# A block of expert_u in one transfer and two buffers instead of two transfers and three buffers; picks worked in place

## Chip, cores and metric

The kernel runs on one core of a Trainium2 chip. The metric is the device time of one execution in microseconds (us); a kernel's time is the median of its runs.

## What is computed

One inference step of a one-layer hybrid decoder: adaLN, an input projection, dilated attention on eight heads and RWKV-7 on eight others, an output projection, and then a layer of product-key experts (PEER), which is the part that matters here. For 1024 prompt tokens and 32 sample tokens of width 1024:

```python
q = (hb @ w_pq).reshape(chunk, PEER_HEADS, 2, PEER_HALF)
s = jnp.einsum('nhpc,hpkc->nhpk', q, sub_keys).astype(jnp.float32)
s1, i1 = lax.top_k(s[:, :, 0], PEER_TOPK)
s2, i2 = lax.top_k(s[:, :, 1], PEER_TOPK)
cand = (s1[..., :, None] + s2[..., None, :]).reshape(chunk, PEER_HEADS, PEER_TOPK * PEER_TOPK)
cid = (i1[..., :, None] * PEER_KEYS + i2[..., None, :]).reshape(chunk, PEER_HEADS, PEER_TOPK * PEER_TOPK)
top_s, pos = lax.top_k(cand, PEER_TOPK)
eid = jnp.take_along_axis(cid, pos, axis=-1)
gate = jax.nn.softmax(top_s, axis=-1)
act = jax.nn.gelu(jnp.einsum('nd,nhkd->nhk', hb, expert_u[eid]).astype(jnp.float32), approximate=False)
return jnp.einsum('nhk,nhkd->nd', gate * act, expert_v[eid].astype(jnp.float32))
```

There are 16384 experts; expert_u and expert_v are 64 MB each in float32. All of it is computed in float32.

## The kernel before

The first 1690 us are the projections, attention, RWKV and the picks of most tokens. The program then works on two things at once.

**The dense loop** (`dense`) treats prompt tiles 0 to 4 (640 tokens) by running all 16384 experts in 128 blocks of 128. `hidden(b)` loads a block of expert_u, transposed, as two halves of [128, 512] floats into the tile u (three buffers of 2 KB a partition), through SP's queue. `split2` makes two float32r operands of each half: ACT casts it to uh, and POOL subtracts, ul = u - uh. uh and ul have two buffers, each for a whole block. PE then multiplies the block with the tokens (h2T), 48 matmuls of 320 columns; ACT takes the gelu, DVE multiplies with the gates g, which SP loads for four blocks at a time (two loads of 640 KB to a group, in rows of 512 B), and ch and cl are the split result. Four blocks are a group. `values` loads a half of the width of expert_v for four blocks (v, two buffers of 2 KB a partition) and splits it into vh (ACT) and vl (POOL, every eighth on DVE), with five buffers each; `output` sums a group's four blocks for one token tile and half of the width, 12 matmuls of 512 columns, and DVE adds the result to dacc. There are ten outputs to a group and 32 groups. In the last group an output is followed by its end: SP loads x1 into the tile fx (which shares the tag and so the buffers of u), DVE multiplies with a gate and adds, SP stores to y.

**The routed tiles**, 5, 6, 7 and the sample tile, take only the experts picked for each token. Their scores come from `route_scores` (weights wq_d through the tile w, five buffers for the tiles 6, 7 and sample), the picks from `route_pick`, and then 832 gathers (`gathered`), each an indirect DMA that POOL issues, of 128 rows of 4 KB of expert_u or expert_v into one of five buffers of the tile row. DVE takes the dot products with expert_u, and sums the rows of expert_v (into gh or ga).

`route_pick` turns the indices of the two top-16 lists into floats (fi, tile tf), adds them to codes cid (tile td), takes the top 16 (tile tt) with their places pu (tile tp), shifts the places into pf (tile te), and subtracts on POOL to find the picked code (tile tq).

The order on each engine is set before the run by the framework's scheduler, which goes by priorities, buffers and its own costs: the gathers and routed tiles are woven with the dense loop, and a change of a buffer count can move instructions of all engines. Each engine then works strictly in that order, and a DMA on SP that waits for a buffer holds all that stand behind it. In the profile every operation has line 196, the recording layer, so instructions go by their tiles' names.

## Time and profile before

| | |
|---|---|
| runs, us | 3748.92, 3759.01, 3769.43; median 3759.01 |
| profiled execution, us | 3753.1 |
| its span, us | 3751.3 |
| mean granted TensorE clock | 0.967 |
| PE busy | 3453.9 us (92%) |
| DVE busy | 2693.2 us (72%) |
| POOL busy | 2080.6 us (55%) |
| ACT busy | 1431.2 us (38%) |
| DMA | 981.58 MB, mean 262 GB/s |

The span is the time from the first to the last instruction of the execution that was profiled; its own time is 1.8 us longer. Shares are means over the span, and the stages have different limits: the dense loop, about 2050 us, has PE and the DMA engines both busy over nine tenths, so what ends each wait there has to be read from that stretch. PE's time is kept apart from that of its weight loads (PEld), which overlap with the matmuls. A busy PE includes the tail of a matmul in the pipeline, and the granted clock is either whole (2.4 GHz) or half of it, so a mean of 0.99 in a stretch is a few us at the lower level.

### The profile page before, as it was taken

The numbers are of one execution on the slowest core, as the hardware profiler recorded it, in microseconds if no ns is written. First come the engines' busy times: TensorE is split into PE (matmuls) and PEld (weight loads), VectorE is DVE, ScalarE is ACT, GpSimd is POOL, SyncE is SP. The second block draws the span as 40 slices with busy tenths as digits, with TensorE's granted clock in tenths as the row PEclk, the third lists the DMA queues.
The fourth block names the chain that finished last, engine by engine and source line by source line (L and its number), as shares of the span: only waits on it lengthen the run. The fifth ranks groups of instructions, "written<-read, shape, count | busy, mean of one in ns | idle before, by whom it ended". The sixth has DMA issues, their size and how long they took to land.

```text
span 3751.3 us, 57270 instructions
## 1 busy us (share of the span) xinstructions
PE 3453.9 (92%) x19618; PEld 2873.9 (77%) x19618; DVE 2693.2 (72%) x6059; ACT 1431.2 (38%) x3122; POOL 2080.6 (55%) x1842
## 2 busy tenths in 40 slices
PE   7999999789888988988999989999999999999998
PEld 3878678567767755556777778988888888898997
DVE  2556365588688656785778998787777877777787
ACT  5645345336765754543221122322223222222321
POOL 2342011015545446754655677777777777776784
PEclk8999999899999989998999999999999999999999
DMA  9653596553675568749988779999999999999997
GB/s 293 197 148 117 176 285 186 151 182 130 225 233 166 189 229 255 244 149 309 320 316 298 262 255 334 340 321 322 327 323 324 329 320 322 315 330 318 336 336 256
DMA packets 592528, 981.58 MB, mean 262 GB/s; under 512 B 78323, under 2 KB 354620, under 8 KB 589420
## 3 DMA queue, kind: packets, MB, share of 16 engines
q1 hardware_dynamic: 467788, 524.84, 43.9%
q0 software_dynamic: 124448, 453.08, 34.1%
q8 instruction: 155, 2.54, 0.3%
q14 instruction: 137, 1.12, 0.1%
HBM read 882.97 MB, written 94.78 MB: 261 GB/s over the span
## 4 chain that ended last, share of the span: by engine, by line
PE 51%; DMA 18%; DVE 14%; issue 7%; POOL 6%; ACT 3%; SPq 1%; POOLq 0%; DVEq 0%; ACTq 0%
PE d L196 23%; PE at L196 10%; PE rw L196 5%; PE pj L196 5%; DMA u<-in_uT 5%; PE rs L196 3%; POOL row L196 3%; DMA row<-in_expert_v,eid 3%; PE sp L196 2%; POOL vl L196 2%; DVE gh L196 2%; DVE ohb L196 1%; DMA v<-in_expert_v 1%; DMA w<-wq_d 1%; POOL ul L196 1%
## 5 line engine op out<-in xcount | busy, mean ns | idle before, releaser
L196 PE MATMUL d<-h2T,uh 128*128 128x320 f32 x4096 | 907.3, 311 | 18.1 <-DVE cl L196 9.0
L196 PEld LDWEIGHTS d<-h2T,uh 128*128 128x128 f32 x4096 | 689.6, 189 | 26.6 <-ACT h2T L196 8.2
L196 PE MATMUL d<-h2T,ul 128*128 128x320 f32 x2048 | 633.3, 311 | 0.6 <-POOL ul L196 0.6
L196 PE MATMUL d<-vl,ch 128*128 128x512 f32 x1280 | 508.3, 398 | 42.9 <-POOL vl L196 42.9
L196 DVE CUSTOM_DVE_ANT_0 row<-row,gh 128x1024 f32<-128x1024 f32 x416 | 500.4, 1215 | 63.5 <-DMA row<-in_expert_u,eid 50.7
L196 POOL DMA_INDIRECT row<-in_expert_u,eid x416 | 394.7, 949 | 242.0 <-DVE co L196 89.6
L196 PE MATMUL d<-vh,cl 128*128 128x512 f32 x1280 | 504.5, 395 | 0.0
L196 PE MATMUL d<-vh,ch 128*128 128x512 f32 x1280 | 478.3, 396 | 17.2 <-DVE cl L196 9.7
L196 POOL DMA_INDIRECT row<-in_expert_v,eid x416 | 397.1, 955 | 166.2 <-issue 46.2
L196 POOL TENSOR_SCALAR oha<-c_iota,tr 128x128 f32<-128x128 f32 x320 | 307.4, 966 | 312.1 <-PE sp L196 293.6
L196 POOL TENSOR_TENSOR ul<-u,uh 128x512 fp32r<-128x512 f32 x256 | 332.2, 1306 | 151.7 <-ACT uh L196 143.3
L196 ACT CAST vh<-v 128x512 fp32r<-128x512 f32 x256 | 158.8, 622 | 674.9 <-DMA v<-in_expert_v 451.9
L196 DVE SCALAR_TENSOR_TENSOR gh<-row,co,gh 128x1024 f32<-128x1024 f32 x285 | 366.1, 1285 | 48.6 <-DMA row<-in_expert_v,eid 46.7
L196 PEld LDWEIGHTS d<-h2T,ul 128*128 128x128 f32 x2048 | 386.2, 189 | 5.0 <-issue 3.7
L196 POOL TENSOR_TENSOR wl<-w,wh 128x1024 fp32r<-128x1024 f32 x50 | 123.0, 2461 | 387.2 <-ACT wh L196 326.8
L196 PEld LDWEIGHTS d<-vl,ch 128*128 128x128 f32 x1280 | 244.1, 191 | 108.0 <-POOL vl L196 58.6
L196 POOL TENSOR_TENSOR vl<-v,vh 128x512 fp32r<-128x512 f32 x224 | 289.0, 1301 | 45.7 <-ACT vh L196 42.7
L196 PEld LDWEIGHTS d<-vh,ch 128*128 128x128 f32 x1280 | 242.7, 190 | 77.5 <-DVE dacc L196 12.7
L196 ACT CAST uh<-u 128x512 fp32r<-128x512 f32 x256 | 154.8, 621 | 367.3 <-DMA u<-in_uT 212.2
L196 PEld LDWEIGHTS d<-vh,cl 128*128 128x128 f32 x1280 | 243.9, 191 | 52.8 <-issue 2.5
L196 DVE TENSOR_TENSOR dacc<-dacc,d 128x512 f32<-128x512 f32 x310 | 206.2, 683 | 47.8 <-PE d L196 47.6
L196 DVE TENSOR_TENSOR d<-d,g 128x320 f32<-128x320 f32 x256 | 126.8, 496 | 155.6 <-ACT d L196 142.4
(449 smaller groups left out, 6779.4 us busy)
## 6 DMA issues: line engine op xcount, KB each, us to landing
u<-in_uT SPq DMA_DIRECT2D x256, 256.0 KB
v<-in_expert_v SPq DMA_DIRECT2D x256, 256.0 KB
w<-wq_d SPq DMA_DIRECT2D x224, 256.0 KB
g_d<-stage SPq DMA_DIRECT2D x20, 2048.0 KB
g<-g_d SPq DMA_DIRECT2D x64, 640.0 KB
w<-in_w_in SPq DMA_DIRECT2D x75, 512.0 KB
w<-in_w_out SPq DMA_DIRECT2D x112, 256.0 KB
adaw<-in_ada_w SPq DMA_DIRECT2D x32, 512.0 KB
```

Of the source, the lines that this page charges most:

```text
L196: return f(*a, **k)
```

## The change

A block of expert_u comes in one transfer of [128, 1024] floats, 4 KB a partition, into two buffers (8 KB in place of 6). ACT's casts and POOL's subtractions stay in halves. The end of the last group, whose fx has the same tag, then has two buffers too. `route_pick` keeps the float indices in the place of the integer ones (ti) and the shifted places in pu, so tiles tf and te go. The scores of the tiles 6, 7 and sample have four buffers for w in place of five.

```diff
@@ -1420,7 +1420,7 @@
         nh = H if i < NT else 2
         v, iu = (x[i][:, :2 * nh] for x in tops)
         eid, gate = (x[i][i][:, :TOPK * nh] for x in (eids, gates))
-        fi = pa.tile([128, 16, TOPK], FT, tag="tf", name="tf", bufs=1)[:, :2 * nh]
+        fi = iu.bitcast(FT)
         ve.tensor_copy(fi, iu)
         v4 = v.rearrange("p (h a) k -> p h a k", a=2)
         f4 = fi.rearrange("p (h a) k -> p h a k", a=2)
@@ -1450,8 +1450,8 @@
         for h in range(nh):
             ve.max_index(pu[:, h, 8:], top[:, h, 8:], r[:, h])
         yield
-        pf = pa.tile([128, H, TOPK], I32, tag="te", name="te", bufs=1)[:, :nh]
-        ve.tensor_scalar(pf, pu.bitcast(I32), 14, None, op0=OP.logical_shift_left)
+        pf = pu.bitcast(I32)
+        ve.tensor_scalar(pf, pf, 14, None, op0=OP.logical_shift_left)
         sh = [128, TOPK, NCAND]
         eqs = []
         for h in range(nh + 1):
@@ -1623,11 +1623,11 @@
         def hidden(b):
             uh = pa.tile([128, KD, 128], FR, tag="uh", name="uh", bufs=2)
             ul = pa.tile([128, KD, 128], FR, tag="ul", name="ul", bufs=2)
+            u = pa.tile([128, KD, 128], FT, tag="u", name="u", bufs=2)
+            sy.dma_start(u, A["uT"][b])
             for x in range(2):
                 ks = slice(4 * x, 4 * x + 4)
-                u = pa.tile([128, 4, 128], FT, tag="u", name="u", bufs=3)
-                sy.dma_start(u, A["uT"][b, :, ks])
-                split2(u, uh[:, ks], ul[:, ks], 8 + b % 2)
+                split2(u[:, ks], uh[:, ks], ul[:, ks], 8 + b % 2)
             ch = pa.tile([128, n], FR, tag="ch", name="ch", bufs=NG + EARLY)
             cl = pa.tile([128, n], FR, tag="cl", name="cl", bufs=NG + EARLY)
             for h in range(2):
@@ -1670,7 +1670,7 @@
             if tt == 0:
                 gate2[dh] = pa.tile([128, 512], FT, tag="act", name="g2", bufs=2)
                 sy.dma_start(gate2[dh], _ap(mod_d, 5 * D + 512 * dh, [[0, 128], [1, 512]]))
-            x1 = pa.tile([128, 512], FT, tag="u", name="fx", bufs=3)
+            x1 = pa.tile([128, 512], FT, tag="u", name="fx", bufs=2)
             sy.dma_start(x1, x1_d[i, :, cs])
             ve.tensor_tensor(acc[:, tt, dh], acc[:, tt, dh], gate2[dh], op=OP.mult)
             ve.tensor_tensor(x1, x1, acc[:, tt, dh], op=OP.add)
@@ -1898,7 +1898,7 @@
                 yield from project_out(open_pool(e3, "frontB", side), pp, tiles, x1.get, h2.get, 2)
             tops = open_tops(e2, "tops_B", tiles, side)
             with ExitStack() as e3:
-                yield from route_scores(open_pool(e3, "routeB", side), pp, h2, tops, 5)
+                yield from route_scores(open_pool(e3, "routeB", side), pp, h2, tops, 4)
             pick = open_pick(e2, side)
             for i in tiles:
                 yield from route_pick(pick, tops, i, gp)
```

The scheduler moves instructions with it. Below, u is a half or a whole block of expert_u, v a half-width of expert_v's block, g the gates of four blocks, row a gather's buffer.

On SP, a group in the middle of the dense loop, before:

```order
L196 DMA u<-in_uT 128x512 x2
L196 DMA v<-in_expert_v 128x512 x2
L196 DMA g<-g_d 128x10x128
L196 DMA u<-in_uT 128x512
L196 DMA g<-g_d 128x10x128
L196 DMA u<-in_uT 128x512 x5
L196 DMA v<-in_expert_v 128x512 x6
```

The same place on SP, now:

```order
L196 DMA u<-in_uT 128x1024
L196 DMA v<-in_expert_v 128x512 x2
L196 DMA g<-g_d 128x10x128
L196 DMA u<-in_uT 128x1024
L196 DMA g<-g_d 128x10x128
L196 DMA u<-in_uT 128x1024 x2
L196 DMA v<-in_expert_v 128x512 x7
```

Before, the second half of the block whose first half is the second of the leading two stands between the two g; now both its halves are ahead of the first g, the next block is between the two, and two blocks come behind the second.

On POOL, the end of the program (ul and vl are the subtractions of u and v), before:

```order
L196 DMA row<-in_expert_v,eid_18712 128x1024 x2
L196 TENSOR_TENSOR vl<-v,vh 128x512
L196 DMA row<-in_expert_v,eid_18712 128x1024 x2
L196 TENSOR_TENSOR vl<-v,vh 128x512
L196 DMA row<-in_expert_v,eid_18712 128x1024
L196 TENSOR_TENSOR ul<-u,uh 128x512 x2
L196 DMA row<-in_expert_v,eid_18712 128x1024
L196 TENSOR_TENSOR vl<-v,vh 128x512
L196 DMA row<-in_expert_v,eid_18712 128x1024 x2
L196 TENSOR_TENSOR vl<-v,vh 128x512 x3
```

The end of POOL's program, now:

```order
L196 DMA row<-in_expert_v,eid_18680 128x1024 x3
L196 TENSOR_TENSOR vl<-v,vh 128x512
L196 TENSOR_TENSOR ul<-u,uh 128x512
L196 DMA row<-in_expert_v,eid_18680 128x1024
L196 TENSOR_TENSOR ul<-u,uh 128x512
L196 TENSOR_TENSOR vl<-v,vh 128x512
L196 DMA row<-in_expert_v,eid_18680 128x1024 x12
L196 TENSOR_TENSOR vl<-v,vh 128x512 x2
L196 DMA row<-in_expert_v,eid_18680 128x1024 x2
L196 TENSOR_TENSOR vl<-v,vh 128x512
```

Before, three gathers follow the last ul; now 14 do, 12 of them ahead of three of the last four vl.

On SP, the end of the program (fx is x1 of the last group, out_y_p its result), before:

```order
L196 DMA out_y_p<-fx 128x512
L196 DMA fx<-x_d 128x512
L196 DMA v<-in_expert_v 128x512
L196 DMA fx<-x_d 128x512
L196 DMA out_y_p<-fx 128x512 x2
L196 DMA fx<-x_d 128x512 x2
L196 DMA out_y_p<-fx 128x512 x2
L196 DMA fx<-x_d 128x512
L196 DMA out_y_p<-fx 128x512
L196 DMA fx<-x_d 128x512
L196 DMA out_y_p<-fx 128x512 x2
```

The end of SP's program, now:

```order
L196 DMA fx<-x_d 128x512
L196 DMA out_y_p<-fx 128x512
L196 DMA fx<-x_d 128x512
L196 DMA out_y_p<-fx 128x512
L196 DMA fx<-x_d 128x512
L196 DMA out_y_p<-fx 128x512
L196 DMA out_y_p<-fx 128x1024
L196 DMA out_y_p<-fx 128x512
L196 DMA fx<-x_d 128x512 x2
L196 DMA out_y_p<-fx 128x512 x2
```

Loads and stores of fx now alternate, and the last two loads stand behind the store of the last routed tile (128x1024), which stood ahead of all of them.

## Rows read from the trace of the kernel before

**Rows 1.** Stretches: us, busy us (instructions) by engine, clock, DMA share, GB/s.

```profile
2250.00:3600.00 1350.00, 1302.57 (x7189) 1171.36 (x7188) 1046.36 (x1514) 375.67 (x753) 1007.28 (x936) 0.99 0.94 326
1690.00:3751.00 2061.00, 1963.34 (x10617) 1722.38 (x10617) 1604.72 (x2727) 550.25 (x1095) 1439.94 (x1330) 0.98 0.91 314
```

**Rows 2.** Waits, 2250 to 3600: who waited <- for whom: us, times, longest.

```profile
ACT uh L196 <- DMA u<-in_uT: 182.8, 57, 10.5
...
POOL ul L196 <- ACT uh L196: 100.7, 41, 6.8
...
PEld d L196 <- POOL vl L196: 52.8, 35, 3.3
...
PE d L196 <- POOL vl L196: 38.7, 28, 2.9
```

**Rows 3.** POOL's instructions, 2250 to 3600: count, busy us, mean ns, idle before.

```profile
L196 POOL DMA_INDIRECT row<-in_expert_v,eid x298 | 284.0, 953 | 99.8 <-issue 37.0 <-DVE gh L196 22.5 <-DVE co L196 18.8
L196 POOL DMA_INDIRECT row<-in_expert_u,eid x288 | 273.5, 950 | 127.1 <-DVE co L196 38.8 <-issue 34.5 <-DVE ga L196 32.7
L196 POOL TENSOR_TENSOR ul<-u,uh 128x512 fp32r<-128x512 f32 x186 | 240.2, 1299 | 107.5 <-ACT uh L196 100.7 <-PE d L196 4.6
...
L196 POOL TENSOR_TENSOR tq<-td,te 128x800 int32<-128x800 int32 x2 | 3.0, 1534 | 0.0
```

**Rows 4.** SP in order of time, one group: start us, us, what, count.

```profile
2772.20 0.38 SPq L196 DMA_DIRECT2D g<-g_d  x1
2772.99 1.18 SPq L196 DMA_DIRECT2D u<-in_uT  x1
2775.15 0.38 SPq L196 DMA_DIRECT2D g<-g_d  x1
2775.62 19.81 SPq L196 DMA_DIRECT2D u<-in_uT  x5
```

**Rows 5.** ACT in order of time, same group; idle time before in brackets.

```profile
2781.43 0.62 ACT L196 CAST uh<-u 128x512 fp32r<-128x512 f32 x1 [5.85 <-DMA u<-in_uT]
...
2790.66 0.62 ACT L196 CAST uh<-u 128x512 fp32r<-128x512 f32 x1 [5.35 <-DMA u<-in_uT]
```

**Rows 6.** POOL in order of time, same group.

```profile
2791.37 1.29 POOL L196 TENSOR_TENSOR ul<-u,uh 128x512 fp32r<-128x512 f32 x1 [6.11 <-ACT uh L196]
...
2798.69 2.49 POOL L196 TENSOR_TENSOR vl<-v,vh 128x512 fp32r<-128x512 f32 x2
```

**Rows 7.** Stretches: a slow group and a fast one.

```profile
2774.00:2835.00 61.00, 57.52 (x311) 51.25 (x311) 45.11 (x78) 15.54 (x32) 43.39 (x41) 0.97 0.91 314
2894.00:2950.00 56.00, 56.00 (x316) 50.99 (x315) 45.85 (x66) 16.45 (x33) 43.26 (x41) 1.00 0.97 341
```

**Rows 8.** Waits in the slow group, 2774 to 2835.

```profile
POOL ul L196 <- ACT uh L196: 6.8, 2, 6.1
```

**Rows 9.** Waits in the fast group, 2894 to 2950.

```profile
POOL ul L196 <- ACT uh L196: 2.7, 3, 1.2
```

**Rows 10.** DMA queues, 2250 to 3600: packets, MB, share of 16 engines.

```profile
q0 software_dynamic: 84300, 306.95, 63.7%
q1 hardware_dynamic: 114221, 131.91, 29.8%
```

**Rows 11.** PE's instructions, 1850 to 2250: the routed tiles' scores.

```profile
L196 PE MATMUL at<-w,x1B 128*128 128x256 f32 (+1 forms) x384 | 89.7, 386 | 0.0
```

**Rows 12.** The tile row: ns min/median/max, first and last start us.

```profile
L196 POOL DMA_INDIRECT row<-in_expert_v,eid x416: 932/940/1357, 2055.7 to 3707.5; - x139
```

**Rows 13.** SP in order of time, the end.

```profile
3740.20 2.15 SPq L196 DMA_DIRECT2D out_y_p<-fx  x2
3743.02 0.33 SPq L196 DMA_DIRECT2D fx<-x_d  x1
```

**Rows 14.** DVE in order of time, the end.

```profile
3746.09 0.69 DVE L196 TENSOR_TENSOR fx<-fx,dacc 128x512 f32<-128x512 f32 x1 [2.31 <-DMA fx<-x_d]
3747.63 0.69 DVE L196 TENSOR_TENSOR fx<-fx,dacc 128x512 f32<-128x512 f32 x1 [0.85 <-DMA fx<-x_d]
```

**Rows 15.** The tile u: ns min/median/max, first and last start us.

```profile
L196 POOL TENSOR_TENSOR ul<-u,uh x256: 1263/1297/3362, 1702.6 to 3702.3; 128x512 fp32r<-128x512 f32 x128
```

## Prediction, made before the changed kernel ran

> **What bounds the kernel now.** I read the table of stretches first, then the waits of the dense stretch, then one group of it instruction by instruction. Everything up to about 1690 us keeps its order on PE, ACT and SP in the changed program (POOL and DVE only rename tiles there), so the argument is about the last 2060 us [rows 1], and above all about the stretch from 2250 to 3600 us, where nothing but the dense expert loop and the row gathers runs.
>
> In that stretch PE is busy 1302.57 of 1350 us at a mean granted clock of 0.99, the DMA engines are busy 0.94 of the time at 326 GB/s, POOL 1007 us [rows 1]. So PE has 47.4 us of idle time there, and the clock takes 0.01 of 1350 us, 13.5 us, more. POOL subtracts 186 halves of expert_u in it, 8 to a group of four blocks, so it holds 23.25 groups of 58.1 us each [rows 3]. Who ends PE's idle time: 38.7 us of it wait for POOL's vl (the low part of expert_v), and not one row of weight for u [rows 2]. Taken alone this says that u does not matter. But POOL works in order, and in front of its vl stand its own ul. POOL waits 100.7 us for ACT's uh, and ACT's uh waits 182.8 us for the transfer of u [rows 2], that is 4.3 and 7.9 us in each group.
>
> One group shows the path. SP issues a g (640 KB) at 2772.20, a half of u at 2772.99, a g at 2775.15, and the next halves from 2775.62 on [rows 4]. ACT gets the first of these halves at 2781.43 after 5.85 us of idle time, the next at 2790.66 after 5.35 us [rows 5]. POOL sits 6.11 us until that cast is through, then has to pass ul, a gather, ul and three gathers, and reaches vl only at 2798.69 [rows 6]. In that group PE is busy 57.52 of 61 us at clock 0.97; in another, from 2894 to 2950, 56.00 of 56 us at 1.00 [rows 7]. POOL's wait for uh is 6.8 us in the one, 2.7 us in the other [rows 8, 9]. Both have u late; PE pays only where POOL is held long. So the late u is bought back on POOL, and what is left over PE pays as a wait for vl and a fall of the clock to its lower level (1.2 GHz) behind it.
>
> **The change part by part.**
>
> *Depth and order of u.* Before, a half is asked for when the half three places earlier has been subtracted; now a whole block when the block two places earlier has. For a first half that is the same moment. For a second half it is earlier, by one block's first ul. The order on SP shows what that is worth: before, the second half of a block stands behind the first g, and the next block's halves behind both; now one whole block stands ahead of the first g and the next between the two. In the group above the half that came at 2781.43 and stalled ACT by 5.85 us would have been asked for before the g of 2772.20. The next block still stands behind one g instead of two. I take it that about two thirds of POOL's 4.3 us in a group go. By the pair of groups, 4.1 us less wait on POOL went with 5 us of a group; so 2.9 us less would be worth 3.5 us, 81 us over 23.25 groups, more than there is. The cap is what PE loses behind vl: 38.7 us of idle time and 13.5 us of clock, 52 us; the floor is 0, if another wait of the same queue takes over (POOL's own gathers: 226.9 us of idle time stand before them [rows 3]). The nearer row is the fast group, which moves 341 GB/s at a DMA share of 0.97 [rows 7] and so shows that the transfers can keep up with 56 us. I take 60% of the cap: **-31 us** (0 to -52).
>
> *Packets of 4 KB for 2 KB.* The queue of SP spends 29.8% of 16 engines on 131.91 MB, the gathers' queue, whose packets are 4 KB rows, 63.7% on 306.95 MB [rows 10]: over 1350 us that is 48.8 and 44.8 us of one engine per MB. The 186 halves are 48.8 MB; if they went from the one price to the other, 195 us of one engine, 12 us of all sixteen, would be saved in 1350 us, 17 us over all 128 blocks; at the other end nothing, since g's short packets carry part of the 48.8. None of it is on PE's path by itself: it makes room in a queue that is busy 0.94. It is in the 31 us; **0** by itself. The Trainium skill (Perfetto Trace Analysis, DMA Optimizations) says that transfers of 4 KB in place of 2 KB can raise throughput dramatically; the two rows leave 8% at most, and by the rule the sum would stand near the -52 end.
>
> *128 transfers fewer on SP*, each some 0.3 to 0.4 us of its time: SP is not waited for as an engine, only for what it queues behind a wait. Now a block's transfer waits for the second ul of the block two before, and behind it on SP stand a g and the v transfers. Those v wait for POOL's vl or ul anyhow, later in the same order. **0**, and if that cover were gone, the -31 above shrinks; it is no term of its own.
>
> *The picks in place.* The cast, the shift and the sums keep their number, shapes and places on DVE; only the tile is another. ti is now held until the last sum for cid, tp until the last of POOL's subtractions, each 1.53 us [rows 3]. The next writer of either is the next tile's pick or scores, which wait for the pick before them already. **0**; if the cover failed, eight subtractions, 12 us, per pick, for three late picks beside dense work.
>
> *Four buffers for wq_d in the routed tiles' scores, not five.* PE has no idle time before these 384 matmuls, 89.7 us in 32 pieces, 2.8 us each [rows 11]. One buffer less asks for a piece at least 2.8 us later, beside dense work that PE has between. From 0 to eight times 2.8, 22 us, if each of the eight rounds lost one piece; the zero row is the nearest: **+1**.
>
> *The gathers stand later on POOL.* The order puts them some 9 subtractions further behind the dense loop from about 2250 us on, and at the end 12 of them stand between the last set's first vl and its other three, and 14 behind the last ul; before, 3. Now the last gather is issued at 3707.5 and the program ends at 3751.3 [rows 12]. A group is half hidden matmuls, half outputs by columns (192 of 320, 120 of 512), so 28 us of its 56 are outputs; the last set of v is needed only after the first 14 us of them and the rest of a hidden block, 3.5 to 7 us. The twelve take 12 x 0.95 = 11.4 us if only POOL limits them, or at the stretch's pace of 1350 / 586 = 2.30 us, 27.6 us [rows 3]. Two vl and two gathers more, and the cover of 17.5 to 21 us is passed by 0 to 12 us. DVE has these rows among the outputs' sums too. **+4** (0 to +12).
>
> *Two buffers for fx, which share the tag of u.* A store issued at 3740.20 frees the buffer of a load at 3743.02 [rows 13], whose sum starts at 3746.09 after 2.31 us of idle time, and the last one waits 0.85 us [rows 14]: 5.9 us from store to sum. With two buffers PE's ten outputs (2.8 us each) come every 5.6 us to a buffer that takes 5.9 + 0.7. One microsecond lost per pair, five pairs, of which 3.2 are lost already: **+2** (0 to +5).
>
> Sum: -31 + 1 + 4 + 2 = **-24 us**. The profiled execution took 3753.1 us (span 3751.3), so 3729; the median of the runs shown is 5.9 us higher, so the forecast against it is **3735**. A difference under 0.5%, 18.8 us, can hardly be told from none here; 3740 and 3778 are the bounds.
>
> **The rivals.**
>
> *The transfers are all one pool, and nothing is gained.* The DMA engines are busy 0.94, and what u gets earlier the gathers get later; POOL then waits longer in front of its gathers for free rows, in the place of its wait for uh, and vl is as late as before. For it: 226.9 us of idle time in front of gathers already; against it: the fast group, which moves 341 GB/s at 0.97 [rows 7]. Time: 0 + 7 = 3760, or 3766 against the median, less up to 9 us for the packets: about 3760. The Trainium skill says so as a rule (DMA: Bandwidth & Descriptors, Issuing engines are not separate DMA queues): what SP and GpSimd issue runs on the same 16 engines and interleaves. The row of 0.94 agrees.
>
> *Slower: the first cast now waits for the second half.* Before, ACT could cast a first half as soon as it had landed. Now both casts of a block wait for 512 KB. The place is ACT's uh and POOL's ul of the two blocks near the g transfers; the price is a half's transfer, 256 KB at 326 GB/s, 0.8 us, for two blocks 1.6 us in a group, which at 5 us per 4.1 is 2 us, and over 23 groups 45 us; half of that, since some are early, 23. It decides once the mean wait of ACT for u exceeds the 7.9 us in a group of now. Then 3753 + 23 + 7 = 3783, against the median 3789. Against it: the block is asked for earlier by more than 0.8 us. The same page of the Trainium skill (Perfetto Trace Analysis, DMA Optimizations) has this rule as well: smaller pieces let some work start sooner.
>
> *All of it:* every group like the fast one, -52 + 7 = -45, 3714 against the median.
>
> That the change doesn't do what it says is excluded by the order: 128 whole transfers stand where 256 halves stood.
>
> **How the numbers follow.** Forecast 0.52 (of which 0.43 below 3740, 0.09 above), all of it 0.10, nothing gained 0.24, slower 0.14. Faster 0.53, within 0.5% 0.33, slower 0.14. The range leaves out the far half of "all of it" and most of "slower": 3702 to 3775. The gain and no change hold 0.86, and the forecast's own range is 3715 to 3748.
>
> **What would show it.** Right: from 2250 us on ACT's wait for u falls under 2.5 us and POOL's for uh under 1.5 us in a group, PE's wait for vl to a third, DMA share 0.96, groups of 56.5 to 57 us. The tail from the start of the last ul, 3702.3 [rows 15], to the end of the span grows from 49 us to 51 to 58. Wrong: POOL's idle time moves to the front of its gathers at the same sum (nothing gained); or ACT's wait for u stays at 7 us or more with whole blocks (slower); or PE waits over 10 us for the last three vl.

## The result, and the profile of the changed kernel

| | before | changed |
|---|---|---|
| median of four runs each, us | 3761.57 (3748.92 to 3769.43) | 3700.85 (3698.76 to 3707.46) |
| ratio, 95% interval | | 0.9845 (0.9814 to 0.9875) |
| span of the profiled execution, us | 3751.3 | 3699.3 |
| mean granted TensorE clock | 0.967 | 0.972 |

The kernel is 1.2 to 1.9% faster, 61 us by the medians and 52 us by the two profiled executions. The forecast was 24 us, and the time lies just under its range of 3702 to 3775: the sign and the main mechanism were right, the size forecast was under half of what came.

The stretches of [rows 1], in the changed kernel (us, busy us and instructions of PE, PEld, DVE, ACT and POOL, clock, DMA share, GB/s):

```profile
2250.00:3600.00 1350.00, 1336.66 (x7484) 1214.61 (x7483) 1086.58 (x1562) 382.76 (x775) 1040.00 (x966) 1.00 0.95 338
1690.00:3699.00 2009.00, 1946.61 (x10654) 1714.69 (x10654) 1601.14 (x2734) 548.56 (x1099) 1440.68 (x1332) 0.99 0.92 323
```

PE's idle time in the dense stretch fell from 47.4 to 13.3 us of 1350 and the clock's mean is 1.00. The waits of [rows 2], same stretch, changed kernel (who <- for whom: us, times, longest):

```profile
ACT uh L196 <- DMA u<-in_uT: 30.0, 16, 3.1
...
PEld d L196 <- POOL vl L196: 14.5, 14, 2.6
POOL ul L196 <- ACT uh L196: 11.9, 8, 2.6
...
PE d L196 <- POOL vl L196: 8.8, 13, 2.2
```

The three waits of the chain all collapsed together: ACT for u from 182.8 to 30.0, POOL for uh from 100.7 to 11.9, PE for vl from 38.7 to 8.8. POOL's instructions, as in [rows 3]:

```profile
L196 POOL DMA_INDIRECT row<-in_expert_v,eid x317 | 302.9, 955 | 120.2 <-issue 47.4 <-DVE gh L196 27.8 <-DVE co L196 23.2
L196 POOL DMA_INDIRECT row<-in_expert_u,eid x288 | 273.6, 950 | 140.6 <-issue 51.2 <-DVE ga L196 39.4 <-DVE co L196 36.8
L196 POOL TENSOR_TENSOR ul<-u,uh 128x512 fp32r<-128x512 f32 x191 | 244.8, 1303 | 16.1 <-ACT uh L196 11.9 <-issue 2.4
```

The idle time before the gathers rose from 226.9 to 260.8 us while that before ul fell from 107.5 to 16.1: the rise is about a third of the fall. There are 605 of them in the same 1350 us, where 586 were. One group, SP and then ACT, to set beside [rows 4, 5]:

```profile
2802.54 0.38 SPq L196 DMA_DIRECT2D g<-g_d  x1
2804.60 0.33 SPq L196 DMA_DIRECT2D u<-in_uT  x1
2809.19 0.38 SPq L196 DMA_DIRECT2D g<-g_d  x1
2809.66 8.92 SPq L196 DMA_DIRECT2D u<-in_uT  x2
```

```profile
2797.89 1.15 ACT L196 CAST uh<-u 128x512 fp32r<-128x512 f32 x2 [0.70 <-PE d L196]
2804.97 1.15 ACT L196 CAST uh<-u 128x512 fp32r<-128x512 f32 x2 [2.00 <-PE d L196]
2814.97 1.14 ACT L196 CAST uh<-u 128x512 fp32r<-128x512 f32 x2 [2.70 <-DMA u<-in_uT]
```

The cast around the first g now waits for PE, no longer for u; only the block between the two g is 2.70 us late, where two halves were 5.85 and 5.35 us late.

**Where the 52 us lie.** The program from 1690 us on splits at three instants that every kernel here has: the first matmul on uh, ACT's 57th cast of u (the routed tiles' scores are done, and their last pick ends at 2260.6 us before and 2262.0 now, a little behind this cast; 24 groups follow) and its 249th (the last group begins).

| stretch, us | before | changed | difference |
|---|---|---|---|
| start to first dense matmul | 1704.0 | 1708.6 | +4.6 |
| **stage**: from there to the 57th cast | 542.5 | 520.7 | -21.8 |
| **loop**: 24 groups, to the 249th cast | 1401.5 | 1354.8 | -46.7 |
| **end**: from there to the end of the span | 103.4 | 115.2 | +11.8 |

The first line is no effect: that part has the same order on PE, ACT and SP in both, and its length is between 1700 and 1717 us in the kernels below. The stage's length is steadier: the kernels below that share an order, all but its last ten us, agree within 1.2 us (542.5 and 542.4 for before and e12; 520.7, 520.0, 519.9 and 521.1 for changed, e4, e7 and e11).

### The profile page after: what moved, and what is told of

Read it like the earlier page. It is cut to its first block, busy times and chain, and to the rows that moved or that the text cites. A ratio compares the mean times of both kernels' runs of the same rounds, so it can differ in the third digit from the quotient of the medians.

```text
span 3699.3 us, 56934 instructions
## 1 busy us (share of the span) xinstructions
PE 3428.0 (93%) x19618; PEld 2861.9 (77%) x19618; DVE 2689.9 (73%) x6059; ACT 1427.1 (39%) x3124; POOL 2081.7 (56%) x1842
## 3 DMA queue, kind: packets, MB, share of 16 engines
q1 hardware_dynamic: 449356, 524.83, 44.2%
## 5 line engine op out<-in xcount | busy, mean ns | idle before, releaser
L196 PE MATMUL d<-h2T,uh 128*128 128x320 f32 x4096 | 906.2, 310 | 10.6 <-ACT h2T L196 7.8
L196 PE MATMUL d<-vl,ch 128*128 128x512 f32 x1280 | 501.4, 392 | 10.4 <-POOL vl L196 10.4
L196 PE MATMUL d<-vh,ch 128*128 128x512 f32 x1280 | 473.5, 392 | 14.5 <-DVE cl L196 6.2
L196 PEld LDWEIGHTS sp<-oha,ohb 128*128 128x128 f32 x1280 | 182.2, 201 | 64.6 <-issue 29.6
L196 PE MATMUL at<-w,h2A 128*128 128x256 f32 x768 | 205.4, 400 | 23.0 <-DMA w<-wq_d 19.0
```

Of the source, the lines that this page charges most:

```text
L196: return f(*a, **k)
```

## Experiments

All ratios are to the kernel before, run beside them on the same chip. A table of the four stretches for all kernels follows at the end of this section.

**How far ahead u is asked for: four halves, and two.** First, the changed kernel with u in four buffers of half a block, each filled by its own transfer of 2 KB a partition (and four for fx):

```diff
-            u = pa.tile([128, KD, 128], FT, tag="u", name="u", bufs=2)
-            sy.dma_start(u, A["uT"][b])
...
+                u = pa.tile([128, 4, 128], FT, tag="u", name="u", bufs=4)
+                sy.dma_start(u, A["uT"][b, :, ks])
```

> The changed kernel with u as four buffers of a half block (2 KB a partition), two transfers a block, in the same 8 KB; all else as changed. Theory of the early request (a second half is asked for one block's subtraction earlier and stands ahead of the first g): the dense stretch is as in the changed kernel, ACT's wait for u from 2250 us on stays under 60 us in 1350, the time is within 10 us of the changed kernel's 3701. Rival, the packets (4 KB rows take a larger share of the DMA engines beside the gathers' 4 KB rows than 2 KB rows do): with 2 KB packets the late u is back, ACT's wait for u is over 120 us and the time is 3735 to 3760.

Measured: 3711.33 us, 0.9863 (0.9822 to 0.9904). The wait for u stayed low with packets of 2 KB, as the early request has it; the time is 10.5 us from the changed kernel's, just past the 10 named, and the stage is 17 us longer. Its waits from 2250 to 3600 us:

```profile
ACT uh L196 <- DMA u<-in_uT: 24.2, 23, 3.3
...
POOL ul L196 <- ACT uh L196: 14.8, 12, 2.3
PE d L196 <- POOL vl L196: 13.6, 13, 2.2
```

Then the dose in the other direction, the kernel before with two halves:

```diff
-                u = pa.tile([128, 4, 128], FT, tag="u", name="u", bufs=3)
+                u = pa.tile([128, 4, 128], FT, tag="u", name="u", bufs=2)
...
-            x1 = pa.tile([128, 512], FT, tag="u", name="fx", bufs=3)
+            x1 = pa.tile([128, 512], FT, tag="u", name="fx", bufs=2)
```

> The kernel before with two buffers of half a block for u in place of three (and two for fx): the dose in the other direction, 256 KB ahead where before had 384 KB and the four halves and the whole blocks have 512 KB. If the early request is what pays, ACT's wait for u in 2250 to 3600 us rises from 182.8 us to 250 to 350, POOL's wait for uh from 100.7 to 130 to 200, a group takes 60 to 62 us and the time is 3780 to 3840. If the transfers are one pool and what u loses the gathers win, the time stays within 10 us of before.

Measured: 3839.01 us, 1.0213 (1.0188 to 1.0238). The same three waits, and the stretch:

```profile
ACT uh L196 <- DMA u<-in_uT: 221.6, 73, 11.1
...
POOL ul L196 <- ACT uh L196: 112.5, 48, 6.4
...
PE d L196 <- POOL vl L196: 70.0, 37, 4.1
```

```profile
2250.00:3600.00 1350.00, 1270.66 (x6892) 1137.97 (x6893) 1001.62 (x1462) 354.67 (x714) 962.10 (x895) 0.97 0.91 314
```

The time is at the upper end of what was expected. A half is 128 x 512 floats, 256 KB, so two, three and four halves are 512, 768 and 1024 KB (the expectation counts them at half of that). With 512, 768 and 1024 KB of u in buffers the loop takes 1462, 1400 to 1417 and 1355 to 1366 us in the kernels of the table below. ACT's and POOL's waits rose little from three halves to two (182.8 to 221.6, 100.7 to 112.5, both by less than was expected), yet PE's wait for vl nearly doubled and the clock fell to 0.97. That POOL has no slack left to take more lateness up would explain it; no run tests this by itself.

**One transfer or two.** The changed kernel, but each whole buffer filled by two transfers:

```diff
-            sy.dma_start(u, A["uT"][b])
+            for x in range(2):
+                sy.dma_start(u[:, 4 * x:4 * x + 4], A["uT"][b, :, 4 * x:4 * x + 4])
```

> The changed kernel, whole blocks in two buffers, but each block filled by two transfers of 2 KB a partition. The order of POOL and of DVE is that of the changed kernel, only SP has 128 transfers more. If the early request and the order are the whole gain, 3695 to 3710, routed stage as short as in the changed kernel (520 us from the first dense matmul to the 57th cast of u), ACT's wait for u 25 to 40 us. If the packets of 4 KB carry part of it (the four halves came 10 us later than the changed kernel), 3708 to 3718, with more PE idle behind vl in every group.

Measured: 3716.85 us, 0.9884 (0.9859 to 0.991), some 15 us more than the changed kernel, and so in the range that was expected if the packets carry part of the gain. ACT's wait for u was 53.5 us, over the 25 to 40 of the other case, and PE's for vl 12.7 (8.8 in the changed kernel). By the profile 9.3 of them lie in the stage, 9.0 in the loop, -1.8 in the end. But its order is not the changed kernel's, as had been assumed: the scheduler moved instructions on all engines. And the loop of one and the same order (the changed kernel, e4 and e7 below differ only at the very end) was 1354.8, 1362.9 and 1355.9 us in three profiles, so 9 us there are within what one order shows; of the three, e4 has waits of 44.5 us for u and 12.5 for vl. SP's queue (packets, MB, share of 16 engines' span) in the changed kernel and in this one:

```profile
q1 hardware_dynamic: 449356, 524.83, 44.2%
```

```profile
q1 hardware_dynamic: 467788, 524.84, 44.6%
```

44.2% of 3699.3 us are 1635 us, 44.6% of 3715.6 are 1657: by this pair, 22 us of all sixteen engines in the whole program for 18,432 packets, give or take 4 by the rounding. But the pair is an extreme one. Worked out in the same way, the seven kernels here with the fewer packets take 1635 to 1653 us, and the ten with the more (e3, with g in another queue, left out) 1645 to 1663: some 9 us apart by the means, with ranges that overlap, for the 17 us at most that [rows 10] allowed. How much of it reaches PE stays open, at most 9 us in the loop.

**Is it g that makes u late?** The kernel before, with g issued by ACT, so that u no longer stands behind it on SP:

```diff
-                    sy.dma_start(G_[h], g_d[n // 64 * h:n // 64 * (h + 1), :, b:b + 4].rearrange("s e i t -> e s i t"))
+                    sc.dma_start(G_[h], g_d[n // 64 * h:n // 64 * (h + 1), :, b:b + 4].rearrange("s e i t -> e s i t"))
```

> The kernel before with one edit: the loads of g are issued by ACT, so that they stand in another queue than u. If u is late because it stands behind two transfers of 640 KB on SP's queue: ACT's wait for u in 2250 to 3600 falls from 183 us to under 60 and the time to 3705 to 3730. If u is late since the DMA engines are busy and its request comes late (the order of the requests, not the queue): the wait stays over 120 us, the time is within 15 us of the kernel before.

Measured: 3763.22 us, 1.0002 (0.9982 to 1.0022). Waits, 2250 to 3600 us, and PE's alone:

```profile
DVE d L196 <- DMA g<-g_d: 79.7, 17, 9.5
...
ACT uh L196 <- DMA u<-in_uT: 57.8, 32, 6.2
...
POOL ul L196 <- ACT uh L196: 31.8, 20, 4.8
```

```profile
PE d L196 <- POOL vl L196: 24.7, 17, 2.4
PE d L196 <- DVE cl L196: 14.2, 6, 4.0
```

DVE's wait for g and PE's for cl in the kernel before, same stretch:

```profile
DVE d L196 <- DMA g<-g_d: 4.9, 2, 3.9
PE d L196 <- DVE cl L196: 4.0, 2, 2.6
```

The mechanism held, u's wait fell from 182.8 to 57.8 us, and yet nothing was gained: g, now issued in its turn behind ACT's casts, came late itself. DVE waited 79.7 us for it (4.9 before) and PE 14.2 us for cl (4.0 before). An expectation missed by leaving out what the moved transfer would wait for.

**The payment.** Before with both payments (picks in place, four buffers of wq_d) and three halves; with the picks alone; with the four buffers alone. The edits are those of the diff above.

> The kernel before with the payment alone: picks in place and four buffers for w in the routed tiles' scores, u as before in three halves. As forecast (w +1, gathers later on POOL +4): 3755 to 3775. Rival, that the 20 us by which the changed kernel is ahead at 2250 us come from the payment and the order it brings: 3735 to 3745, with the first group of the dense loop alone at its place some 20 us earlier.

> The kernel before with the picks worked in place and nothing else (five buffers of wq_d, three halves of u). Both payments together gained 7 us, some 10 of them before 2250 us. If that came from where the picks' work falls among DVE's other work, this kernel shows another order on DVE around 2100 to 2250 us and a stage of 525 to 535 us there (542 before), and 3748 to 3756 in all. If it came from the four buffers of wq_d, the stage is 540 to 545 us and the time that of before within 3 us.

> The kernel before with four buffers of wq_d in the routed tiles' scores and nothing else. Both payments gained 7 us, the picks in place 3 to 5. If the missing buffer costs PE its wait for wq_d, the scores take up to 22 us longer and the time is 3760 to 3780; if PE has dense work there, the stage stays at 535 to 545 us and the time within 5 us of before. The gathers at its end are the 3 of before, so its end is that of before, 101 to 105 us.

Measured: both 3754.1 us, 0.9971 (0.9954 to 0.9988); the picks 3755.51, 0.9991 (0.9972 to 1.0009); the buffers 3768.02, 1.0025 (1.0009 to 1.0041). The two do not add: together they gain 0.29%, 11 us, and the stage is 11 us shorter, half of the 20 that the rival named; the buffers alone lose 0.25%, 9 us, and by their profile that lies in the loop (15.7 us longer), where no w is used. The picks alone have a stage of 538.4 us, between the two ranges expected. Each of the three has its own order. And of these three only the kernel with both has 13 gathers behind the last ul: with either alone there are 3, as before.

**The stage.** At ACT's 41st cast of u the two kernels are still within 3 us of each other (399 us after the first dense matmul before, 402 now); the whole gain of the stage lies in the two groups behind it. Around 2090 to 2250 us DVE is busy 154.51 of 160 us in the kernel before, with the picks of three sets, and PE pauses. The stretch before and in the changed kernel, in the columns of [rows 1]:

```profile
2090.00:2250.00 160.00, 138.88 (x761) 125.53 (x760) 154.51 (x384) 41.58 (x81) 119.18 (x104) 0.96 0.79 256
```

```profile
2090.00:2250.00 160.00, 151.93 (x859) 137.19 (x858) 150.98 (x394) 49.05 (x96) 123.78 (x107) 1.00 0.78 259
```

PE's idle time there, before and in the changed kernel, on the lines of its matmuls:

```profile
L196 PE MATMUL d<-h2T,uh 128*128 128x320 f32 x348 | 79.1, 316 | 9.0 <-DVE cl L196 9.0
...
L196 PE MATMUL d<-vh,ch 128*128 128x512 f32 x80 | 30.9, 408 | 7.5 <-DVE cl L196 5.7 <-DVE dacc L196 1.7
```

```profile
L196 PE MATMUL d<-h2T,uh 128*128 128x320 f32 x373 | 82.2, 310 | 0.0
...
L196 PE MATMUL d<-vh,ch 128*128 128x512 f32 x87 | 33.3, 396 | 7.6 <-DVE cl L196 4.9 <-DVE d L196 1.7 <-DVE dacc L196 0.9
```

Before, one of the pauses on DVE (td are the sums of the codes cid, tt the top scores of a pick; cl is what PE waits for until 2180.80):

```profile
2173.37 4.80 DVE L196 TENSOR_TENSOR td<-tf 128x128 f32<-128x128 f32 x7
2178.09 1.28 DVE L196 SCALAR_TENSOR_TENSOR gh<-row,co,gh 128x1024 f32<-128x1024 f32 x1
2179.29 0.98 DVE L196 MAX8 tt<-tc 128x8 f32<-128x50 f32 x8
2180.19 0.47 DVE L196 TENSOR_TENSOR cl<-d,ch 128x320 fp32r<-128x320 f32 x1
```

Seven us of pick and row sum stand in front of a subtraction (cl) that PE needs. Is it the picks' amount? In both kernels, the second eight of each pick were copied from the first for the tiles 6, 7 and the samples:

```diff
-        for h in range(nh):
-            ve.match_replace(r[:, h], top[:, h, :8], cand[:, h], -3.0e38)
...
-        for h in range(nh):
-            ve.max(top[:, h, 8:], r[:, h])
-        for h in range(nh):
-            ve.max_index(pu[:, h, 8:], top[:, h, 8:], r[:, h])
+            ve.tensor_copy(top[:, :, 8:], top[:, :, :8])
+            ve.tensor_copy(pu[:, :, 8:], pu[:, :, :8])
```

> The kernel before; for the three sets that are picked beside dense work (6, 7 and the samples) the second eight of each head's sixteen picks are copies of the first eight: 24 short instructions a set less on DVE, some 5 us. The output is not the reference's. If the pauses of PE around 2100 to 2250 us come from DVE's picks standing in front of the dense sums, their sum falls from 20 us to under 10 and the stage from the first dense matmul to the 57th cast of u from 542 to 518 to 530 us. If the stage is long for another reason (u late, wq_d late), it stays over 535.

> The changed kernel with the same lighter picks (output not the reference's). By the theory of DVE's order the changed kernel has little left to gain there: pauses 4.6 us to 1 to 5, stage 520 to 508 to 520, so that the stages of before and after stand under 12 us apart where 22 were; if u or the transfers made the stage shorter, they stay 20 apart. 3685 to 3700 in all.

Both missed. Before: 3763.02 us, 1.0009 (0.9988 to 1.0029), stage 543.7. Changed: 3699.03 us, 0.9841 (0.9819 to 0.9862), stage 531.7, longer than with the full picks. PE's waits from 2090 to 2250 us, the first and the second:

```profile
PE d L196 <- DVE cl L196: 10.7, 4, 6.9
```

```profile
PE d L196 <- DVE cl L196: 6.7, 1, 6.7
PE d L196 <- DVE dacc L196: 5.1, 2, 2.7
```

So this much less of the picks' work does not take the pauses away. The dose was small, though: by the pages DVE's busy time fell from 2693.2 to 2687.2 us and from 2689.9 to 2681.0, and each of the two has a new order besides, so a larger cut stays untested. The other half of the theory is the place: the dense loop's gelu, product, split and output sums were put ahead of the picks where the order is made, in both kernels:

```diff
+                with tc.high_priority(offset=AHEAD):
...
-                sc.activation(t, t, AF.Gelu)
+                    sc.activation(t, t, AF.Gelu)
```

> The kernel before with the dense loop's own work on ACT and DVE (the gelu, the product with g, the split into ch and cl, the sums of the outputs) put ahead of the picks and gathers where the order is made; nothing else. If the stage of the routed tiles is long because of where DVE's picks stand in front of these sums, PE's pauses from 2090 us on fall from 20 us to under 10 and the stage from 542 to 518 to 532 us, with u as late as before; the dense groups stay near 58.4 us, so 3740 to 3752. If the stage became short through u, it stays at 538 or more.

> The changed kernel with the same sums ahead. By the theory of the order there is little left: pauses 4.6 us to 2 to 8, stage 512 to 525, dense groups 56 to 57 us, time 3690 to 3708. If the order in the changed kernel was short by chance, any new order costs it some of the 22 us: stage 525 to 540 and 3700 to 3720.

Before: 3753.01 us, 0.998 (0.9962 to 0.9998); the pauses after 2090 us, counting those of 1 us and more, fell from 20.0 to 11.7 us and the stage from 542.5 to 532.3, with u as late as ever (187.4 us from 2250 to 3600) and DVE as busy (154.13 of 160 us). All three lie just outside the ranges expected. Changed: 3704.95 us, 0.9861 (0.9824 to 0.9898), stage 528.6: the new order gave back 8 of the 22 us. So an order alone, at the same depth and the same work, moves the stage by 10 us. That it is the place of the sums which does it is likely and not shown, since e2 has a stage of 531.3 us without it. The order of the changed kernel is a lucky one of its kind.

**The end.** The changed kernel with fx in three buffers of g; the same with the last four subtractions of expert_v on DVE; that and the sums ahead:

```diff
-            x1 = pa.tile([128, 512], FT, tag="u", name="fx", bufs=2)
+            x1 = pa.tile([128, 512], FT, tag="g", name="fx", bufs=3)
...
-                split2(v, vh, vl, b % 8)
+                split2(v, vh, vl, 0 if dh and grp == ngrp - 1 else b % 8)
```

> The changed kernel with x1 of the last group (fx) in the three buffers of the gates g, which are free by then, instead of the two of u. If the two buffers of fx make the end longer (59 us from the last ul to the end, 49 before): 3 to 8 us faster than the changed kernel, 3693 to 3698, and DVE's waits for fx behind 3680 us go. If the end is long because 14 gathers follow the last ul: no change, 3699 to 3705.

> The changed kernel with fx in three buffers of g, and the last four subtractions of expert_v, which stand between the last gathers on POOL, on DVE. If the gathers in front of vl on POOL set the end, the last vl is ready some 8 us earlier than at 3672 to 3678, PE ends at 3668 to 3676, and the time is 3688 to 3695. If the gathers themselves are late (their rows and transfers), DVE's sums of the rows stand in front of vl instead, and the time is that of the changed kernel within 4 us.

> The changed kernel with the sums ahead, fx in three buffers of g, and the last four subtractions of expert_v on DVE. If the parts add, the end (last group's first cast to the end of the span) is 105 to 110 us in place of 115 and the time 3685 to 3698; if each new order costs or gains some 10 us in the routed stage by chance, it lies between 3690 and 3715.

Measured: 3700.62 us, 0.9826 (0.9788 to 0.9864); 3696.19, 0.9833 (0.9807 to 0.9858); 3702.55, 0.985 (0.9816 to 0.9884). None is told apart from the changed kernel by these intervals, though all four runs of the second (3689.71 to 3698.17) lie below the changed kernel's lowest, 3698.76. In the second the last vl was through at 3669.8 us in place of 3673.6, and yet PE ended at 3679.4 us (3680.3 in the changed kernel): it waited 3.5 us for DVE's sums into dacc instead, which stand among the sums of the same gathers. The third lies in the range expected if each new order costs or gains some 10 us by chance.

Last, 64 of the 128 rows of expert_v of tile 5 left out, so that no gather stands behind the last ul, in the changed kernel and in that before:

```diff
-        yield from sum_rows(gat, acc, dots[eid.tensor.name], eid, 128)
+        yield from sum_rows(gat, acc, dots[eid.tensor.name], eid, 64 if i == 5 else 128)
```

> The changed kernel; the tokens of tile 5 sum 64 of their 128 rows of expert_v, 64 of 832 gathers less, so that the last gather stands before the last groups' subtractions (output not the reference's). If the gathers at the end are what makes the end longer, the time from the last group's first cast to the end of the span falls from 115 us to 92 to 102, and the whole to 3675 to 3690. If the sums of fx in two buffers set it, PE ends earlier but the end stays at 108 us or more.

> The kernel before with the same 64 rows less (output not the reference's): its end has only a few gathers, so it falls from 103 us to 92 to 102 and the two ends, 12 us apart, come within 5 of each other if the gathers are the cause, and stay 10 apart if fx is.

Measured: 3694.99 us, 0.9825 (0.9806 to 0.9843), end 104.3; and 3757.74, 0.9994 (0.9979 to 1.001), end 95.8. The end of the changed kernel fell by 11 us, not to the 92 to 102 expected, and the time to none of the 3675 to 3690: in this profile the loop took 11 us more. The two ends stay 8.5 us apart. Of that, some 4.5 us are where the count starts: in e12 the last group's first cast came later in PE's work, with 210 hidden matmuls still to do (241 in e11), 31 less at some 7 us for 48. About 4 us are left, which is the difference in the last column of the table below.

**All kernels by stretch**, from their profiles. Pauses: PE's idle time between matmuls in the stage, those over 0.3 us. Late gathers: those behind the last ul on POOL. The last column is from PE's last matmul of the dense loop to the end of the span.

| kernel | u in buffers | stage | pauses | loop | end | late gathers | fx buffers | after PE |
|---|---|---|---|---|---|---|---|---|
| e5 two halves | 512 KB | 557.4 | 35.7 | 1462.0 | 105.5 | 0 | 2 | 14.2 |
| before | 768 KB | 542.5 | 24.9 | 1401.5 | 103.4 | 3 | 3 | 11.4 |
| e2 both payments | 768 KB | 531.3 | 14.7 | 1402.2 | 109.9 | 13 | 3 | 15.8 |
| e8 picks | 768 KB | 538.4 | 23.8 | 1401.9 | 103.9 | 3 | 3 | 11.6 |
| e16 four w | 768 KB | 538.6 | 19.2 | 1417.2 | 101.2 | 3 | 3 | 11.4 |
| e3 g on ACT | 768 KB | 538.9 | 21.3 | 1400.0 | 107.2 | 3 | 3 | 11.5 |
| e9 light picks | 768 KB | 543.7 | 23.5 | 1403.3 | 101.3 | 3 | 3 | 11.5 |
| e12 fewer rows | 768 KB | 542.4 | 22.6 | 1413.5 | 95.8 | 0 | 3 | 10.6 |
| e13 sums first | 768 KB | 532.3 | 19.8 | 1409.7 | 105.3 | 11 | 3 | 13.1 |
| changed | 1024 KB | 520.7 | 9.3 | 1354.8 | 115.2 | 14 | 2 | 19.0 |
| e1 four halves | 1024 KB | 538.0 | 18.9 | 1361.6 | 100.8 | 9 | 4 | 10.4 |
| e6 two transfers | 1024 KB | 530.0 | 13.7 | 1363.8 | 113.4 | 14 | 2 | 19.1 |
| e4 fx in g | 1024 KB | 520.0 | 8.9 | 1362.9 | 109.0 | 14 | 3 | 13.2 |
| e7 last v on DVE | 1024 KB | 519.9 | 9.4 | 1355.9 | 110.2 | 14 | 3 | 14.5 |
| e10 light picks | 1024 KB | 531.7 | 14.9 | 1358.9 | 104.3 | 5 | 2 | 14.5 |
| e11 fewer rows | 1024 KB | 521.1 | 10.2 | 1365.7 | 104.3 | 0 | 2 | 14.6 |
| e14 sums first | 1024 KB | 528.6 | 13.4 | 1356.0 | 112.0 | 14 | 2 | 18.9 |
| e15 all | 1024 KB | 524.7 | 11.0 | 1360.9 | 109.8 | 14 | 3 | 14.3 |

## Why the prediction was right or wrong

Two steps failed. The share of the loop's loss that would come back was put at 60% of the cap where 90% came (-46.7 us for -31), and the new order on DVE in the stage was put at nothing, by the words that the picks keep their places there, where it went with -21.8 us.

**Depth and order of u: right in mechanism, a third too small.** It is the largest term: -46.7 us in the loop for -31. Eight kernels with 768 KB of u take 1400 to 1417 us there (mean 1406), nine with 1024 KB take 1355 to 1366 (mean 1360), with whole blocks and halves alike, so -46 is not a number of one profile; the payments without the depth (e2) leave the loop at 1402.2. The step that failed is the share: I took two thirds of POOL's wait and 60% of the cap of 52 us. No row stood behind the 60%, and the pair of groups, at 81 us, was already past the cap. POOL's wait for uh fell by 88%, and 90% of the cap was had. What I held back was the block between the two g, and it is 2.70 us late in the group above; POOL could take up that much, as the fast group [rows 7, 9] with 2.7 us of wait for uh and no loss on PE had shown. That row was the forecast for the loop, and "all of it" (3714), to which I gave 0.10, was nearer than my 3735: groups of 56.45 us, where the fast one took 56.

**The stage: missed altogether, and the larger error.** I forecast +1 there, from wq_d alone, and it gave -21.8. Of this 15.6 us are fewer pauses of PE; the rest goes with the clock (0.97 to 0.98 over 1690 to 2250 us, 5.6 us). The prediction says of the picks that "the cast, the shift and the sums keep their number, shapes and places on DVE", and looks for a cost only. But the change gives every engine a new order in the 160 us in which DVE has under 6 us to spare, and PE waits there for cl and dacc from DVE. Which share depth has in it is not settled: orders with 768 KB take 531 to 544 us, orders with 1024 KB 520 to 538, means some 10 apart with ranges that overlap, and 512 KB takes 557. With both payments in all of them, e2 takes 531.3 with 768 KB and the nine with 1024 KB 520 to 538, so there the depth by itself is not seen. That an order moves 10 us with u unchanged is shown by e13; that the order of the changed kernel is 8 us better than one with the sums ahead is shown by e14, whose expectation left both open. No rule was found by which one could have read the 22 us from the order alone.

**The payments: 0 and +1.** No cost of their own was found: e2 has a stage 11 us shorter than before. Four buffers alone, +9 us in all, lose it in the loop by their profile, and it is of the size that a new order gives.

**The end: right in where it lies, half the size, and partly by another wait.** +11.8 for +6. The two parts can be read from the last column of the table, from PE's last matmul to the end: with three buffers of fx and few late gathers 10.6 to 11.6 us, with three and 13 or 14 gathers 13.2 to 15.8, with two and few 14.2 to 14.6, with two and 14 gathers 18.9 to 19.1. So two buffers cost 3 to 6 us where +2 was forecast, and late gathers cost 2 to 5 there. Ahead of that, from the last group's first cast to the last matmul, kernels with 13 or 14 late gathers take 93 to 96 us and those with few mostly 85 to 92, some 4 us more. What I priced, a late vl, cost PE little; from 3590 us to the end it waited:

```profile
PE d L196 <- DVE dacc L196: 1.9, 2, 1.6
PE d L196 <- POOL vl L196: 1.6, 2, 1.4
```

The gathers were thus undersized because I counted only their delay of vl (+4), not that of DVE's sums, before and behind PE's last matmul. The range of that term was too narrow as well: 14 gathers at 2.30 us and two vl at 1.3 are 34.8 us, which pass the cover by 14 to 17 us and not by 12. In the changed kernel, POOL at the end:

```profile
3654.78 0.94 POOL L196 DMA_INDIRECT row<-in_expert_v,eid  x1 [0.62 <-DVE gh L196]
3656.57 1.14 POOL L196 DMA_INDIRECT row<-in_expert_v,eid  x1 [0.86 <-DMA row<-in_expert_v,eid]
3658.96 1.14 POOL L196 DMA_INDIRECT row<-in_expert_v,eid  x1 [1.25 <-DVE gh L196]
3661.95 1.14 POOL L196 DMA_INDIRECT row<-in_expert_v,eid  x1 [1.85 <-DVE gh L196]
3663.11 2.56 POOL L196 TENSOR_TENSOR vl<-v,vh 128x512 fp32r<-128x512 f32 x2
3665.82 1.23 POOL L196 DMA_INDIRECT row<-in_expert_v,eid  x1 [0.16 <-issue]
3671.12 1.14 POOL L196 DMA_INDIRECT row<-in_expert_v,eid  x1 [4.07 <-DVE gh L196]
3672.28 1.27 POOL L196 TENSOR_TENSOR vl<-v,vh 128x512 fp32r<-128x512 f32 x1
```

The longest of these waits are for DVE to sum an earlier row, DVE has the dense loop's last sums too, and the last vl stands behind the last gather. On DVE, the last fx, to set beside [rows 14]:

```profile
3689.83 0.69 DVE L196 TENSOR_TENSOR fx<-fx,dacc 128x512 f32<-128x512 f32 x1 [0.75 <-DMA fx<-x_d]
3693.95 0.69 DVE L196 TENSOR_TENSOR fx<-fx,dacc 128x512 f32<-128x512 f32 x1 [3.42 <-DMA fx<-x_d]
3695.56 0.69 DVE L196 TENSOR_TENSOR fx<-fx,dacc 128x512 f32<-128x512 f32 x1 [0.92 <-DMA fx<-x_d]
```

5.09 us of idle time for the transfers where 3.16 were before. e4 takes the two buffers away and gains 6 us in this column; in the time of the whole it can't be seen.

**Packets of 4 KB: 0 by itself.** Four halves and whole blocks in two transfers, both in packets of 2 KB, have nearly the loop of the changed kernel: 1361.6 and 1363.8 against 1354.8 to 1362.9 us. The rule of the Trainium skill (Perfetto Trace Analysis, DMA Optimizations) that 4 KB in place of 2 KB can raise throughput dramatically is not what happened here: the share of SP's queue was 44.2% with the one and 44.6% with the other, and the whole of the loop's gain but for 9 us at most comes without it. The sum that it would have given, near -52, is close to what came, and yet e1 and e6 have most of it with packets of 2 KB.

**The rivals.** "One pool, nothing gained": the rule of the Trainium skill that stood behind it (DMA: Bandwidth & Descriptors, Issuing engines are not separate DMA queues) agrees with the rows, since the gathers' idle time did rise by 34 us as u's fell by 91; but a third is not all, the share had room from 0.94 to 0.95 and the rate from 326 to 338 GB/s, and the gathers are not what PE waits for in the loop. (The up to 9 us that this rival took off for the packets is worked out nowhere; the rows gave 12 to 17.) "Slower, since the first cast waits for the second half": ACT's wait for u fell to a sixth, so it fell too: every kernel of the table with whole blocks has a shorter loop than every one with three halves.

**What would show it.** The signs that I named for the mechanism came: ACT's wait for u 1.3 us in a group (under 2.5), POOL's for uh 0.5 (under 1.5), PE's for vl under a quarter (a third), share 0.95 (0.96). Groups came at 56.45 us, just below the 56.5 to 57 named. The end, from the last ul (3639.9 us) to 3699.3, is 59.4 us, above the 51 to 58. None of the signs of being wrong came: PE waited 1.6 us, not over 10, for the last vl.

## What to carry to other kernels

When a late load stalls an engine in order and the loss appears two engines further on, take the fastest instance of the loop in the trace as the forecast of the repaired loop, once its rates show that the transfers can keep up; shaving a "cautious" share off it, with no row for the share, was the error here. A change of buffer counts in a kernel whose order is made by a scheduler changes the order everywhere: where an engine is nearly full (DVE, 154.51 of 160 us) such a new order was worth up to 18 us at the same buffers for u, more than most of the terms that can be argued, and the range has to carry it for every stage that is reordered. And moving a transfer to another queue moves its lateness with it: ask first what will stand ahead of it there.

## What the runs showed of the hardware that was not expected

The same 128 blocks in packets of 4 KB in place of 2 KB saved little: SP's queue took 1635 to 1653 us of all sixteen DMA engines in the kernels with whole transfers and 1645 to 1663 with halves, some 9 us apart by the means, and with the DMA engines busy 0.95 of the time the loop's length hardly depends on it. And what u's lateness cost PE did not grow in proportion: from three halves to two, ACT's wait for u rose by 21% and PE's for vl by 81%, with the granted clock at 0.97 for 0.99.
